# Where the Gram matrices of a gated delta rule are made, and how the blocks of its triangular solve reach the chip's memory

## The chip, the core and the metric

The kernel runs on one core of a Trainium2 chip. The metric is the device time of one execution in microseconds (us), from the first to the last instruction of the core. The engines are named as in the profile: PE (matrix products; PEld loads its weights), DVE (vector), ACT (scalar functions), POOL (GpSimd) and SP, which here only issues DMAs; ACT and POOL issue some too. TensorE's granted clock has two levels, 1.2 and 2.4 GHz.

## What is computed

A decoder layer on 1024 tokens of width 2048, all float32. After an RMS norm one projection feeds two groups of heads: a gated delta rule (8 heads of 128) and a sparse attention (8 query heads, 2 key/value heads) that keeps 256 keys per query by the scores of an indexer. Their gated outputs go through one output projection; the input is added, and a last RMS norm ends it. The change is in the delta rule, which works by blocks:

```
q = l2_normalize(q) * dk**-0.5 ;  k = l2_normalize(k)
gc    = cumsum(g)                                   # log decay inside a block
decay = where(incl, exp(gc_i - gc_j), 0)
lmat  = where(strict, (k * beta) @ k.T * decay, 0)  # "Gram", strictly lower
tmat  = inverse(lmat + eye)                         # the solve
w, u  = tmat @ (k * beta * exp(gc)), tmat @ (v * beta)
# then block after block: v_new, o and the state
```

Blocks here have 128 tokens. Each block's inverse is put together from two 64 x 64 diagonal blocks, which are solved directly, and the block below the diagonal.

## The kernel before

The activations h^T stay on chip, split into two exact parts (`hT`), and every projection is a slab of 256 columns (`slab_cm`, product at L286). A slab has 8 pieces of weights; a piece is loaded by SP (`wraw`, L200, three buffers), split by ACT (`whi`, L191) and POOL (`wlo`, L192, two buffers each) and gives 24 matmuls of 512 columns into four PSUM banks. There are 5664 such matmuls in all, in this order: small columns, four slabs of the indexer, five of the attention's queries and keys (`proj_qk`), four of the delta rule's keys ("k"), four of its queries ("q"), four of its values ("v"), four gate slabs of the attention and four of the delta rule. The output projection follows (L1276 to L1303).

A scheduler orders each engine's instructions when the program is built, by priorities: weights first, then the emptying of banks, then side work, then projection matmuls. Side work therefore stands between projection matmuls wherever the scheduler expects its inputs. On the chip each engine takes its instructions strictly in the order so made.

Side work, in its order: the indexer's scores; the choice of the 256 keys (`tally`, tiles `tj`, `cand`, `hit`, `key`; L652 to L681), a long chain on DVE during the last query slabs and the first two key slabs; attention (`attend`: logits `lgp`, then `pT`, `po`), which needs that choice and lies in the key, query and first value slabs; then the delta rule's part that needs no values; last the recurrence over the eight blocks (`delta_rule`).

A key, query or value slab (`proj_conv`) empties each of its banks with ACT into a stage tile `xr` (four buffers). ACT, DVE and POOL make the causal convolution and SiLU in place (`cy`, L700 to L705). In the next slab `tokens` transposes the result on PE (`ctok`, L711, in the trace under the helper L150) into the one PSUM bank with the tag "ev"; ACT reads it, for keys four times with a running sum of squares (`ssk`) and four times into the tile that goes to DRAM. The channels-first tile also goes to DRAM (`cT`).

The part that needs no values comes after attention, in tiles of memory that attention gave back. `pipelined` goes over 16 units of a block of 128 tokens and four heads. `gram_load` has SP load the keys (`kT`, L910) and the rows of gc, repeated on every partition (`gcb`, L905). `gram_unit` makes four products on PE (L916), four Relu and one Exp on ACT (L918, L919), a triangular select on POOL (L920), and four DVE operations (L922) that scale the product by `cn` = -beta rk^2 and by the decay; SP stores the result (`Ms`, L924). After both units of a block `block_load` (L932) has SP read the two diagonal 64 x 64 blocks of all eight heads back, one block per partition, in rows of 256 bytes. `solve` inverts all 128 blocks at once on DVE in 62 steps of two operations (`ut`, `mb`; L941, L943). `combine` makes the block below the diagonal, for which SP reads `L2bd` from `Ms` (L965).

A gate slab (`proj_gate`) empties a bank in two steps: ACT writes a tanh to a stage tile (`sz`, L1114), then DVE reads that tile and the bank (L1115).

## Time and profile before

| | us |
|---|---|
| median of 3 runs | 2167.59 |
| lowest and highest run | 2165.65, 2169.2 |
| span of the profiled execution | 2165.4 |

The page gives no other time of the profiled execution than its span. Busy shares of that span: PE 96%, PEld 81%, DVE 60%, ACT 40%, POOL 29%. The page cuts the span in 40 slices of 54.1 us and gives a digit for each, in tenths. A matmul's busy time has its pipeline in it, so that two that follow each other overlap in the records. "x <- y" after an idle time says what ended it.

### The profile page before, as it was taken

To read this page: it belongs to the slowest core of one execution; us is meant where nothing else is said; L and a number is where in the kernel's file an instruction comes from. 1 tells how busy PE (TensorE), PEld (TensorE's weight loads), DVE (VectorE), ACT (ScalarE), POOL (GpSimd) and SP (SyncE) were. 2 spreads that over 40 slices of the span, in tenths; PEclk is the share of its full clock that TensorE was granted. 3 is DMA by queue.
4 is the path that set the end of the run, shared out by engine and by line. 5 is a ranking of instruction groups with operands and counts; after the bars stand their busy time and mean duration, and the time that the engine had idled before them with its cause. 6 is when DMAs were issued, how large, how long until landed. Compare 5 with 4: busy or idle time off the path is not lost.

```text
span 2165.4 us, 30374 instructions
## 1 busy us (share of the span) xinstructions
PE 2084.5 (96%) x10529; PEld 1754.1 (81%) x10529; DVE 1293.9 (60%) x2751; ACT 872.3 (40%) x2054; POOL 637.9 (29%) x696
## 2 busy tenths in 40 slices
PE   7999999999999999999999978899999999999998
PEld 6888887877887888888888866778889877777887
DVE  8626766899999656545555426992154454445335
ACT  7425544211133655545545543112355433334223
POOL 6443334555532211112112222222233221111211
PEclk9999999999999999999999999999999999999999
DMA  6222232222223332222222395126565474556434
GB/s 191 72 71 78 71 81 78 65 77 68 70 80 112 111 88 87 73 78 81 67 72 74 108 199 106 61 80 169 167 195 182 136 252 136 160 160 223 140 121 157
DMA packets 258699, 248.93 MB, mean 115 GB/s; under 512 B 61888, under 2 KB 208752, under 8 KB 258096
## 3 DMA queue, kind: packets, MB, share of 16 engines
q1 hardware_dynamic: 205296, 187.19, 30.5%
q0 software_dynamic: 10240, 33.56, 5.1%
q10 hardware_dynamic: 43008, 26.22, 4.0%
q8 instruction: 83, 1.36, 0.3%
q14 instruction: 72, 0.59, 0.1%
HBM read 185.66 MB, written 61.24 MB: 114 GB/s over the span
## 4 chain that ended last, share of the span: by engine, by line
PE 53%; DVE 21%; DMA 5%; issue 2%; ACT 2%; SPq 1%; POOL 0%; DVEq 0%; ACTq 0%; POOLq 0%
PE cm L286 26%; PE to L1276 13%; DVE tj L652 8%; DVE mb L943 3%; DVE ut L941 3%; PE lgp L147 2%; PE po L147 2%; PE pT L150 1%; PE tl L1303 1%; DVE cy L702 1%; PE tm L238 1%; DMA Ms<-M 1%; DMA kT<-cTk 1%; PE ctok L150 1%; DVE sw L456 1%
## 5 line engine op out<-in xcount | busy, mean ns | idle before, releaser
L286 PE MATMUL cm<-hT,whi 128*128 128x512 f32 (+1 forms) x3776 | 1212.1, 396 | 16.4 <-DVE sz L1115 11.5
L286 PEld LDWEIGHTS cm<-hT,whi 128*128 128x128 f32 (+1 forms) x3776 | 709.1, 189 | 162.1 <-DVE sz L1115 13.7
L286 PE MATMUL cm<-hT,wlo 128*128 128x512 f32 (+1 forms) x1888 | 748.7, 397 | 5.3 <-POOL wlo L192 5.2
L192 POOL TENSOR_TENSOR wlo<-wraw,whi 128x512 fp32r<-128x512 f32 (+1 forms) x248 | 336.6, 1358 | 887.4 <-ACT whi L191 869.0
L286 PEld LDWEIGHTS cm<-hT,wlo 128*128 128x128 f32 (+1 forms) x1888 | 357.5, 189 | 80.2 <-POOL wlo L192 9.1
L191 ACT ACTIVATE whi<-wraw 128x512 fp32r<-128x512 f32 (+1 forms) x256 | 159.0, 621 | 456.8 <-PE cm L286 329.5
L1276 PE MATMUL to<-whi,mx 128*128 128x512 f32 x896 | 281.2, 395 | 5.2 <-DVE sz L1115 2.6
L1276 PEld LDWEIGHTS to<-whi,mx 128*128 128x128 f32 x896 | 169.2, 189 | 46.1 <-ACT whi L225 3.2
L652 DVE TENSOR_SCALAR_CACHE_REDUCE tj<-score,cand 128x384 bf16<-128x384 f32 (+2 forms) x198 | 187.1, 945 | 6.6
L1276 PE MATMUL to<-wlo,mx 128*128 128x512 f32 x448 | 176.1, 395 | 4.0 <-DVE wlo L226 4.0
L226 DVE TENSOR_TENSOR wlo<-wraw,whi 128x512 fp32r<-128x512 f32 x112 | 77.0, 690 | 145.3 <-ACT whi L225 145.1
L509 DVE SCALAR_TENSOR_TENSOR score<-rl,wi,score 128x512 f32<-128x512 f32 (+3 forms) x150 | 127.5, 859 | 30.1 <-ACT rl L501 23.5
L221 POOL DMA_DIRECT2D wraw<-in_w_out_dram x112 | 60.4, 539 | 255.3 <-DVE wlo L226 229.5
L225 ACT ACTIVATE whi<-wraw 128x512 fp32r<-128x512 f32 x112 | 70.1, 629 | 156.5 <-PE to L1276 132.2
L702 DVE SCALAR_TENSOR_TENSOR cy<-xr,convw,cy 128x512 f32<-128x512 f32 x144 | 119.9, 833 | 21.6 <-ACT cy L700 20.0
L794 DVE CUSTOM_DVE_ANT_0 lg<-lgp,mk 128x512 f32<-128x512 f32 (+3 forms) x96 | 53.2, 555 | 88.5 <-PE lgp L147 87.5
L1276 PEld LDWEIGHTS to<-wlo,mx 128*128 128x128 f32 x448 | 85.0, 190 | 23.7 <-DVE wlo L226 4.8
L813 DVE TENSOR_TENSOR pT<-pT 128x512 fp32r<-128x512 f32 (+1 forms) x80 | 49.7, 634 | 68.8 <-ACT pT L812 68.7
L501 ACT ACTIVATE rl<-isc 128x512 f32<-128x512 f32 (+1 forms) x105 | 58.9, 572 | 55.3 <-PE isc L147 30.9
L147 PE MATMUL po<-pT,vv 128*128 128x256 f32 x432 | 72.2, 285 | 0.0
L941 DVE TENSOR_TENSOR ut<-mb 128x62 f32<-128x62 f32 (+30 forms) x62 | 62.9, 1015 | 13.6 <-DMA mb<-Ms 11.8
L147 PEld LDWEIGHTS po<-pT,vv 128*128 128x128 f32 x432 | 65.2, 189 | 6.8
(280 smaller groups left out, 2614.4 us busy)
## 6 DMA issues: line engine op xcount, KB each, us to landing
wraw<-in_w_in_dram SPq DMA_DIRECT2D x232, 256.0 KB, 2.9
wraw<-in_w_out_dram POOLq DMA_DIRECT2D x128, 256.0 KB, 3.2
xt<-in_x_dram SPq DMA_DIRECT2D x32, 256.0 KB, 4.8
kT<-cTk SPq DMA_DIRECT2D x32, 256.0 KB, 3.1
szT<-sz SPq DMA_DIRECT2D x32, 256.0 KB, 2.1
mx<-oT SPq DMA_DIRECT2D x32, 256.0 KB, 4.1
mx<-szT SPq DMA_DIRECT2D x32, 256.0 KB, 6.3
ox<-in_x_dram SPq DMA_DIRECT2D x30, 256.0 KB, 3.2
```

The source lines that it names most:

```text
L147: return anchored(PE.matmul(*a, **k))
L191: S.activation(whi[:, :, :ncol], raw[:, :, :ncol], AF.Copy)
L192: eng.tensor_tensor(wlo[:, :, :ncol], raw[:, :, :ncol], whi[:, :, :ncol].bitcast(F32), op=ALU.subtract)
L225: last_w[:] = [S.activation(whi, raw, AF.Copy), V.tensor_tensor(wlo, raw, whi.bitcast(F32), op=ALU.subtract)]
L226: V.tensor_tensor(wlo, raw, whi.bitcast(F32), op=ALU.subtract)]
L286: mms.append(PE.matmul(bank[:n, :], w[:, k, g * P:g * P + n], h_ap(kt, a, slice(h * HT, h * HT + HT)), start=(p == 0 and k == 0 and i == 0 ...
L509: V.scalar_tensor_tensor(dst, r, w1, dst, op0=ALU.mult, op1=ALU.add)
L652: V.tensor_scalar(junk[:, :(b + 1) * P], score[b], cand[:, i:i + 1], 0.0, op0=op, op1=ALU.add, accum_out=cnt[:, i:i + 1])
L702: V.scalar_tensor_tensor(y, xr[:, j:j + HT], convw[:, j, ch:ch + 1], y, op0=ALU.mult, op1=ALU.add)
L941: V.tensor_tensor(tv, u[:, j + 1:, j:j + 1].to_broadcast([P, n, j]), u[:, j:j + 1, :j].to_broadcast([P, n, j]), op=ALU.mult)
L943: V.tensor_tensor(u[:, j + 1:, :j], u[:, j + 1:, :j], tv, op=ALU.add)
L1276: PE.matmul(banks[j], m_ap(KTS[m], a, slice((4 * hf + j) * P, (4 * hf + j + 1) * P)), ws[m][w], start=(m == 0 and i == 0), stop=(m == D // ...
```

## The change

- `decay_units` makes exp(gc_i - gc_j), strictly lower, for the 16 units, and keeps it in DRAM (`dec`). Its instructions are issued by `w_piece`: with each of the pieces 1 to 5 of a slab, from the first query slab of the attention on, one slot is taken from the list `per_piece`; a slot loads one unit's rows of gc and makes the decay of the unit before. The first Relu of a unit stands behind that piece's weight split on ACT. The tile `gce` has two buffers.
- `tokens` of a key slab loads the decay of its head and four blocks on SP (`decay_load`), and after the transposes `gram` makes the four products from the channels-first tile that is still on chip, into the bank with the tag "ev". It works `cn` out from the sums of squares at hand (three small DVE operations), scales with four DVE operations in place, and SP stores the two diagonal blocks to `Md`, in the order in which the solve takes them, and the block below the diagonal to `L2s`.
- `block_load` is four loads of 32 partitions by 16 KB, issued on ACT's queue; `combine` reads `L2s`.
- The loop over the units, `gram_load`, `gram_unit`, `pipelined` and `Ms` are gone; `cn` is no longer made after the key slabs; the two scratch tiles of `rsqrt` in the pool `gp` have one buffer instead of two.

```diff
+    per_piece = []
@@ w_piece
-            w_split(whi, wlo, raw, ncol, V if w2d is w_out else G)
+            ins = w_split(whi, wlo, raw, ncol, V if w2d is w_out else G)
+            if per_piece and 1 <= p <= 5:
+                per_piece.pop(0)(ins)
@@ proj_conv
+        def decay_load(f, h):
+            E = gcp[0].tile([P, NCH, P], F32, tag="gce", name="gce", bufs=2)
+            SP.dma_start(E, dec[:, f * NCH:(f + 1) * NCH, h, :])
+            return E
+
+        def gram(f, h, o, E):
+            cs = slice(f * NCH, (f + 1) * NCH)
+            pg = sd.tile([P, 512], F32, tag="ev", name="gram", bufs=1)
+            for c in range(NCH):
+                PE.matmul(pg[:, c * P:(c + 1) * P], o[:, c * P:(c + 1) * P], o[:, c * P:(c + 1) * P], start=True, stop=True)
+            r2 = gcp[0].tile([P, NCH, 1], F32, tag="gr2", name="gr2", bufs=2)
+            V.tensor_scalar(r2, ssk[:, cs, h:h + 1], 4 * EPS, None, op0=ALU.add)
+            V.reciprocal(r2, r2)
+            V.scalar_tensor_tensor(cn[:, cs, h:h + 1], r2, -1.0, beta[:, cs, h:h + 1], op0=ALU.mult, op1=ALU.mult)
+            for c in range(NCH):
+                V.scalar_tensor_tensor(E[:, c, :], pg[:, c * P:(c + 1) * P], cn[:, f * NCH + c, h:h + 1], E[:, c, :],
+                                       op0=ALU.mult, op1=ALU.mult)
+            for q in range(2):
+                sl = slice(64 * q, 64 * q + 64)
+                SP.dma_start(Md.rearrange("(q c h) r j -> q h r c j", q=2, h=HEADS)[q, h, :, cs, :], E[sl, :, sl])
+            SP.dma_start(L2s[:, cs, h, :], E[64:128, :, 0:64])
@@ block_load
-    def block_load(mb, c):
-        for q in range(2):
-            sl = slice(64 * q, 64 * q + 64)
-            SP.dma_start(mb[part(c, q):part(c, q) + HEADS], Ms[c][sl, :, sl].rearrange("r h j -> h r j"))
+    def block_load(mb):
+        for i in range(4):
+            sl = slice(32 * i, 32 * i + 32)
+            S.dma_start(mb[sl], Md[sl])
@@ order of the work
+    def decay_units():
...
+        def load(c, g):
+            def fn(ins):
+                E[c, g] = gcp[0].tile([P, 4, P], F32, tag="gce", name="gce", bufs=2)
+                SP.dma_start(E[c, g], gcrow[c * HEADS + 4 * g:c * HEADS + 4 * g + 4, :][None, :, :].to_broadcast([P, 4, P]))
+            return fn
+
+        def make(c, g):
+            def fn(ins):
+                t = E[c, g]
+                for h in range(4):
+                    r = S.activation(t[:, h, :], t[:, h, :], AF.Relu, bias=ngc[:, c, 4 * g + h:4 * g + h + 1])
+                    if h == 0:
+                        after(r, ins)
+                S.activation(t, t, AF.Exp, scale=-1.0)
+                G.affine_select(t, t, [[0, 4], [-1, P]], ALU.is_gt, 0.0, base=0, channel_multiplier=1)
+                SP.dma_start(dec[:, c, 4 * g:4 * g + 4, :], t)
+            return fn
...
+        per_piece.extend(slot(n) for n in range(len(units) + 1))
...
-        with tc.tile_pool(name="g1a", bufs=1, reuse_waits="tile") as g1a:
-            def unit(c, g, *a):
-                gram_unit(g1a, c, g, *a)
-                if g == 1:
-                    block_load(mb, c)
-            pipelined(UNITS, lambda c, g: gram_load(g1a, c, g), unit, 2)
+        block_load(mb)
```

How the engines' orders change, at three places. A row is one instruction, or several alike that follow each other: the line, the operation, out<-in, the output's shape. Line numbers of the changed kernel are its own.

DVE at the end of the choice of keys: `mk` of 384 columns is the last mask, `kT` and `qaT` are the keys and queries that attention's first logits take; before:

```order
L680 SCALAR_TENSOR_TENSOR mk<-eq,mk 128x384
L702 SCALAR_TENSOR_TENSOR cy<-xr,convw,cy 128x512 x3
L705 SCALAR_TENSOR_TENSOR xr<-xr,cy 128x512
L745 TENSOR_TENSOR kT<-kT 128x512 x2
L777 TENSOR_TENSOR qaT<-qaT 128x256 x2
```

and with the change:

```order
L736 SCALAR_TENSOR_TENSOR gce<-gram,cn,gce 128x128 x4
L692 SCALAR_TENSOR_TENSOR mk<-eq,mk 128x384
L714 SCALAR_TENSOR_TENSOR cy<-xr,convw,cy 128x512
L717 SCALAR_TENSOR_TENSOR xr<-xr,cy 128x512
L732 TENSOR_SCALAR gr_7437<-ssk 128x4
L733 RECIPROCAL gr_7437<-gr_7437 128x4
L734 SCALAR_TENSOR_TENSOR cn<-gr_7437,beta 128x4
L783 TENSOR_TENSOR kT<-kT 128x512 x2
L815 TENSOR_TENSOR qaT<-qaT 128x256 x2
```

Ahead of the split of keys and queries there are now, counted over the whole order, six sets of the three small operations and five sets of four that scale a Gram product. On PE the first logits stand behind 2373 projection matmuls (2363 before) and attention's last product behind 3963 (3990).

ACT in the query slabs of the attention (`gce` is the decay's tile, first with Relu, then with Exp), with the change:

```order
L194 ACTIVATE whi<-wraw 128x512
L1139 ACTIVATE gce<-gce,ngc 128x128
L1142 ACTIVATE gce<-gce 128x512
L1139 ACTIVATE gce<-gce,ngc 128x128 x3
L194 ACTIVATE whi<-wraw 128x512
```

and SP at the same place:

```order
L1144 DMA dec<-gce 128x512
L480 DMA qkT<-qk 32x512
L1132 DMA gce<-gcrow 128x512
L204 DMA wraw<-in_w_in_dram 128x2x256
L1144 DMA dec<-gce 128x512
```

Before, the weight splits follow each other there, with the emptying of a slab's banks between. Three Relu of a unit now stand ahead of a weight split, the fourth and the Exp behind it; on SP a load of gc's rows into a buffer stands behind the store that empties one.

DVE at the solve (`ut` and `mb` are its two operations of a step); before, at steps 17 and 18 with the first gate slab:

```order
L941 TENSOR_TENSOR ut<-mb 128x782
L1115 SCALAR_TENSOR_TENSOR sz<-sz,cm_12727 128x512
L943 TENSOR_TENSOR mb<-mb,ut 128x46x17
L1115 SCALAR_TENSOR_TENSOR sz<-sz,cm_12728 128x512
L941 TENSOR_TENSOR ut<-mb 128x810
L1115 SCALAR_TENSOR_TENSOR sz<-sz,cm_12729 128x512
```

and with the change at the same steps:

```order
L947 TENSOR_TENSOR ut<-mb 128x782
L949 TENSOR_TENSOR mb<-mb,ut 128x46x17
L947 TENSOR_TENSOR ut<-mb 128x810
L714 SCALAR_TENSOR_TENSOR cy<-xr,convw,cy 128x512
L949 TENSOR_TENSOR mb<-mb,ut 128x45x18
L714 SCALAR_TENSOR_TENSOR cy<-xr,convw,cy 128x512
```

Steps 18 to 27 now hold the convolution of the last value slab, and the first two gate slabs come at steps 32 and 49; before, three gate slabs came at steps 17, 33 and 51, and the last value slab's convolution ended at step 3. On PE the recurrence begins behind 4855 projection matmuls (5028 before) and ends behind 5331 (5511).

## Rows read from the trace of the kernel before

**Rows 1.** The page: busy us (share of the span) xinstructions, and the slices of DMA.

```profile
PE 2084.5 (96%) x10529; PEld 1754.1 (81%) x10529; DVE 1293.9 (60%) x2751; ACT 872.3 (40%) x2054; POOL 637.9 (29%) x696
...
DMA  6222232222223332222222395126565474556434
```

**Rows 2.** Windows: length, busy us (instructions) of each engine, PE clock, DMA share, GB/s.

```profile
650.00:700.00 50.00, 46.91 (x206) 38.13 (x204) 48.90 (x65) 18.26 (x55) 11.84 (x13) 0.97 0.32 98
...
800.00:850.00 50.00, 50.00 (x268) 42.63 (x267) 29.02 (x82) 26.63 (x75) 8.87 (x13) 1.00 0.27 78
...
1250.00:1300.00 50.00, 38.00 (x182) 30.88 (x180) 14.59 (x45) 23.51 (x62) 11.81 (x18) 0.90 0.99 187
1300.00:1350.00 50.00, 41.48 (x177) 33.88 (x178) 29.26 (x49) 15.91 (x40) 11.44 (x10) 0.93 0.57 108
```

**Rows 3.** Groups of PE's matmuls, 1230 to 1340 us: busy, mean ns, idle before.

```profile
L286 PE MATMUL cm<-hT,whi 128*128 128x512 f32 x180 | 60.5, 412 | 4.1 <-ACT whi L191 4.1
L286 PE MATMUL cm<-hT,wlo 128*128 128x512 f32 x90 | 37.5, 416 | 0.4 <-POOL wlo L192 0.4
L887 PE MATMUL gram<-kT 128*128 128x128 f32 x128 | 20.5, 316 | 16.7 <-DMA kT<-cTk 16.7
L150 PE MATMUL ctok<-ident,xr 128*128 128x128 f32 x24 | 4.1, 299 | 0.6 <-DVE xr L705 0.6
```

**Rows 4.** The chain in order of time: start us, us, what.

```profile
1252.59 9.10 DMA Ms<-M
...
1546.02 1.78 PE pa L887 x16
...
1736.11 10.04 PE cm L286 x44
```

**Rows 5.** Groups of PE's matmuls, 1340 to 1460 us, beside the solve.

```profile
L286 PE MATMUL cm<-hT,whi 128*128 128x512 f32 x301 | 98.1, 405 | 11.6 <-DVE sz L1115 11.5
L286 PE MATMUL cm<-hT,wlo 128*128 128x512 f32 x150 | 60.4, 402 | 0.0
```

**Rows 6.** Timeline, PE at the first gate slab beside the solve: start, us, idle before.

```profile
1359.23 0.79 PE L286 MATMUL cm<-hT,whi 128*128 128x512 f32 x1 [6.77 <-DVE sz L1115]
```

**Rows 7.** Timeline, DVE and then PE at attention's first logits.

```profile
704.30 0.96 DVE L777 TENSOR_TENSOR qaT<-qaT 128x256 fp32r<-128x256 f32 x2 [0.16 <-ACT qaT L776]
...
704.32 1.89 PE L147 MATMUL lgp<-kT,qaT 128*128 128x512 f32 x7
```

**Rows 8.** The Gram stage's operations by line: ns min/median/max, first and last start.

```profile
L918 ACT ACTIVATE M<-gcb,ngc x64: 385/388/411, 1234.2 to 1310.0; 128x128 f32<-128x128 f32 x64
...
L919 ACT ACTIVATE M<-M x16: 612/630/635, 1235.5 to 1310.4; 128x512 f32<-128x512 f32 x16
...
L920 POOL TENSOR_SCALAR_AFFINE_SELECT M<-M x16: 636/637/693, 1236.2 to 1311.1; 128x512 f32<-128x512 f32 x16
...
L922 DVE SCALAR_TENSOR_TENSOR M<-gram,cn,M x64: 334/341/351, 1237.4 to 1313.1; 128x128 f32<-128x128 f32 x64
```

**Rows 9.** DMA issues: queue, count, KB each, median us from issue to landing.

```profile
szT<-sz SPq DMA_DIRECT2D x32, 256.0 KB, 2.1
...
gcb<-gcrow SPq DMA_DIRECT2D x16, 256.0 KB, 7.8
Ms<-M SPq DMA_DIRECT2D x16, 256.0 KB, 6.5
...
gcd<-gcrow SPq DMA_DIRECT2D x16, 256.0 KB, 3.7
```

**Rows 10.** 400 to 600 us: all engines; DVE's small operations, 395 to 600; one undisturbed.

```profile
400.00:600.00 200.00, 195.48 (x844) 160.08 (x843) 191.34 (x415) 31.29 (x51) 107.15 (x90) 0.98 0.25 69
...
L661 DVE SCALAR_TENSOR_TENSOR cand<-key,flip 128x6 int32<-128x6 int32 x25 | 14.9, 594 | 0.9
...
L663 DVE TENSOR_SCALAR hit<-cnt 128x6 int32<-128x6 f32 x24 | 10.3, 430 | 0.8
...
609.37 0.17 DVE L663 TENSOR_SCALAR hit<-cnt 128x6 int32<-128x6 f32 x1
```

More of the change, by code (lines that the diff above doesn't have):

```diff
@@ L112, in rsqrt @@
     def rsqrt(pool, y, v, n):
-        t1 = pool.tile([P, n], F32, tag=f"rs1_{n}", name="rs1", bufs=2)
-        t2 = pool.tile([P, n], F32, tag=f"rs2_{n}", name="rs2", bufs=2)
+        bufs = 1 if pool is gp else 2
+        t1 = pool.tile([P, n], F32, tag=f"rs1_{n}", name="rs1", bufs=bufs)
+        t2 = pool.tile([P, n], F32, tag=f"rs2_{n}", name="rs2", bufs=bufs)
         V.tensor_single_scalar(t1.bitcast(I32), v.bitcast(I32), 1, op=ALU.logical_shift_right)
@@ L408, in hybrid_layer @@
     tok = {nm: dr.tile([T, HEADS * P], F32, name="tok" + nm) for nm in "kv"}
+    Md = dr.tile([P, 64, 64], F32, name="Md")
+    L2s = dr.tile([64, NB, HEADS, 64], F32, name="L2s")
+    dec = dr.tile([P, NB, HEADS, P], F32, name="dec")
+    gcp = []
     oT = dr.tile([P, 16, T], F32, name="oT")
@@ L628, in hybrid_layer @@
         cyp = cyp_cm.__enter__()
+        gcp_cm = tc.tile_pool(name="gcp", bufs=1, side="right", reuse_waits="tile")
+        gcp.append(gcp_cm.__enter__())
         with tc.tile_pool(name="tkp", bufs=1, reuse_waits="tile") as tkp, pri(P_SIDE):
@@ L706, in ev @@
             late.append(lambda: tokens(f, h, o))
+        def decay_load(f, h):
[18 more added lines that the diff above has]
+            SP.dma_start(L2s[:, cs, h, :], E[64:128, :, 0:64])
         def tokens(f, h, o):
+            E = decay_load(f, h) if nm == "k" else None
             pt = sd.tile([P, 512], F32, tag="ev", name="ctok", bufs=1)
@@ L716, in tokens @@
                     S.activation(sqj, pt[:, c * P:(c + 1) * P], AF.Square, accum_out=ss[:, f * NCH + c, h:h + 1])
+            if nm == "k":
+                gram(f, h, o, E)
             if nm != "q":
@@ L875, in attention @@
             todo.append(e)
-    Ms = [dr.tile([P, HEADS, P], F32, name=f"Ms{c}") for c in range(NB)]
     TTs = [dr.tile([64, HEADS, 64], F32, name=f"TTs{c}") for c in range(NB)]
@@ L888, in mm4 @@
         return ps.rearrange("p (h j) -> p h j", h=4)
-    def pipelined(units, load, work, ahead):
-        got = {}
-        for n, u in enumerate(units):
-            for m in range(n, min(n + ahead + 1, len(units))):
-                if m not in got:
-                    got[m] = load(*units[m])
-            work(*u, *got.pop(n))
-            got[n] = None
-    UNITS = [(c, g) for c in range(NB) for g in range(2)]
     def gc_rows(pool, tag, c, g, bufs):
@@ L906, in gc_rows @@
         return E
-    def gram_load(g1, c, g):
-        kT = g1.tile([P, 4, P], F32, tag="kT1", name="kT1", bufs=3)
-        SP.dma_start(kT, cT["k"][:, 4 * g:4 * g + 4, c * P:(c + 1) * P])
-        return kT, gc_rows(g1, "gcb", c, g, 3)
-    def gram_unit(g1, c, g, kT, E):
-        M = g1.tile([P, 4, P], F32, tag="M1", name="M1", bufs=3)
-        pg = mm4("gram", kT, kT)
-        for h in range(4):
-            S.activation(M[:, h, :], E[:, h, :], AF.Relu, bias=ngc[:, c, 4 * g + h:4 * g + h + 1])
-        S.activation(M, M, AF.Exp, scale=-1.0)
-        G.affine_select(M, M, [[0, 4], [-1, P]], ALU.is_gt, 0.0, base=0, channel_multiplier=1)
-        for h in range(4):
-            V.scalar_tensor_tensor(M[:, h, :], pg[:, h, :], cn[:, c, 4 * g + h:4 * g + h + 1], M[:, h, :],
-                                   op0=ALU.mult, op1=ALU.mult)
-        SP.dma_start(Ms[c][:, 4 * g:4 * g + 4, :], M)
     def part(c, q):
         return (q * NB + c) * HEADS
-    def block_load(mb, c):
-        for q in range(2):
-            sl = slice(64 * q, 64 * q + 64)
-            SP.dma_start(mb[part(c, q):part(c, q) + HEADS], Ms[c][sl, :, sl].rearrange("r h j -> h r j"))
+    def block_load(mb):
+        for i in range(4):
+            sl = slice(32 * i, 32 * i + 32)
+            S.dma_start(mb[sl], Md[sl])
     def solve(g1, mb):
@@ L1117, in proj_gate, with slot, fn @@
         slab_cm([(c0, CG)], CG, ev, budget=budget)
+    def decay_units():
+        E = {}
+        def load(c, g):
[14 more added lines that the diff above has]
+            return fn
+        units = [(c, g) for c in range(NB) for g in range(2)]
+        def slot(n):
+            def fn(ins):
+                if n < len(units):
+                    load(*units[n])(ins)
+                if n > 0:
+                    make(*units[n - 1])(ins)
+            return fn
+        per_piece.extend(slot(n) for n in range(len(units) + 1))
     kvp_cm = tc.tile_pool(name="kvp", bufs=1, side="right", reuse_waits="tile")
     kvp = kvp_cm.__enter__()
+    decay_units()
     for c in range(4):
@@ L1140, in hybrid_layer @@
     kvp_cm.__exit__(None, None, None)
+    gcp_cm.__exit__(None, None, None)
     proj_conv("v", C_GV, 0)
```

6 lines of the change are left out of this document (3 added, 3 removed).

## The prediction

> **What bounds the kernel now.** I read the page's busy shares and slices first [rows 1]: PE is busy 96% of the span, and the slices of DMA show a 9 and a 5 in places 24 and 25, 1245 to 1353 us, where it is else at 2 to 6. The busy time of a matmul contains its pipeline, so I price PE by spacing instead: 44 projection matmuls with 512 columns take 10.04 us in the chain of waits, 0.228 us each, and 16 of the 128-column fp32 ones 1.78 us, 0.111 us each [rows 4]. By that price a stretch such as 800 to 850 us is full: PE stands at 50.00 of 50, DVE at 29, ACT at 27, POOL at 9 [rows 2]. So almost everywhere the kernel is bound by PE, and a change saves time only where PE has holes.
>
> The largest hole is the Gram stage. Between 1230 and 1340 us PE issued 270 projection matmuls, 128 Gram and 24 transposing ones [rows 3]: 270 x 0.228 = 61.6 and 152 x 0.111 = 16.9, together 78.5 us of work in 110. **31.5 us are lost.** The rows name the wait: 16.7 us before gram for DMA kT<-cTk [rows 3]; the chain has a 9.10 us store Ms<-M [rows 4]; DMA stands at 0.99 and the granted clock at 0.90 in that window [rows 2], so part of the loss is PE running at the lower of its two levels (1.2 instead of 2.4 GHz) after it had idled.
>
> The second hole is beside the solve. Between 1340 and 1460 us PE issued 451 projection matmuls [rows 5], 102.8 us of work in 120: 17.2 us lost. Its waits are for DVE's sz, which reads a gate slab's bank and stands in DVE's order between steps of the solve; the first of them is 6.77 us [rows 6].
>
> **The change part by part.**
>
> *The Gram stage goes.* Its 64 Gram products (128 matmuls in the trace) cost PE the same 0.111 us elsewhere, so only the 31.5 us of waiting go: **-31.5**. With it go 64 loads and stores of 128 to 256 KB at the place where DMA is full. What is late next is the solve's block load: 2 MB in four issues on ACT's queue. At the lowest rate of 1300 to 1350 us, 108 GB/s [rows 2], it takes some 19 us, at the rate of 1250 to 1300, 187 GB/s, 11. That is off PE's path: PE has a whole value slab to do first. ACT's four issues are covered by the lead of one piece that the split weights have (24 x 0.228 = 5.5 us); if that cover went, they would cost about as long as a landing of 2.1 us [rows 9].
>
> *The Gram moves into the key slabs.* Attention's first logits wait for DVE, which is full up to there: 650 to 700 us shows 48.90 of 50 [rows 2]. DVE ended the split query at 705.26 and PE began logits at 704.32 on the first part [rows 7], so today the two meet. The order puts six sets of three small operations and five of four Gram products ahead of the split keys, with as many other operations as before: 18 x 0.2 (a 6-column operation takes 0.17 us [rows 10], with its gap 0.2) + 20 x 0.341 [rows 8] = 10.4 us. PE gets, ahead of the same logits, ten more projection matmuls (2373 instead of 2363) and six sets of four Gram products: 10 x 0.228 + 48 x 0.111 = 7.6 us. The other ten tiles of the Gram come after that, where DVE stands near 29 of 50: nothing, while DVE has that slack; without it each is 4 x 0.341 + 0.6 = 2.0 us, 20 in all.
>
> *The decay moves under the query projections.* Its 16 selects of 0.637 us on POOL [rows 8] add 10.2 us to POOL, which is busy 107 of 200 us there, beside a DVE at 191 [rows 10]. The row on DVE's small operations shows what POOL costs DVE: cand takes 594 ns in the mean and hit 430, where one undisturbed takes 170; 25 x 0.42 + 24 x 0.26 = 16.8 us for 107 us of POOL [rows 10], 0.157 us per us. For 10.2 us more that is 1.6 us. If every select held one DVE operation up for its whole length, it would be 16 x 0.637 = 10.2 us [rows 8]. I take 1.6, because the rows are of this very stretch, and keep 10.2 as a rival. A rule speaks against the change here: the Trainium skill (SBUF — State Buffer, section "Terms") says that DVE and GpSimd arbitrate for a shared port pair, that it is held for the whole instruction and that the loser fully blocks. By that rule the term would be the 10.2; the trace agrees that DVE's small operations wait beside POOL (594 for 170 ns), not that each POOL instruction meets one. Logits then come 10.4 + 1.6 - 7.6 = **+4.4** us of PE's time later.
>
> ACT's part of a decay, 4 x 0.388 + 0.630 = 2.18 us [rows 8], stands between two weight splits, with loads and stores ahead of it on SP, and it has two buffers. A store (2.1, as szT), a load (3.7, as gcd), ACT 2.18 and POOL 0.64 [rows 8, 9] make a loop of 8.6 us for every second decay; PE gives it two pieces, 2 x 5.47 = 10.9 us. So I take 0. With the landings of the crowded Gram stage, 6.5 and 7.8 [rows 9], the loop is 17.1 us; that end is the rival on the slower side. DMA stands at 0.25 here [rows 10], which is near the lower end. SP's waits for a store's landing hold the weight loads behind them, which run three buffers ahead.
>
> *Bank hand-over.* Of the third and fourth key slabs the last bank now comes right behind a Gram product, whose tile must be given back before ACT (0.6 us) can empty the bank. One of these lies ahead of the logits and is inside the 4.4; the other I put at **+1** (0 to 3).
>
> *The solve.* It starts about a value slab earlier. DVE now has the last value slab at its steps 18 to 27 and two gate slabs at 32 and 49, where before three gate slabs stood at 17, 33 and 51. A value slab's bank is emptied by ACT alone, so one of three waits goes: 17.2 / 3 = 5.7, taken as **-5**. Bounds: all 17.2 gone, or, if the solve starts late against the order, a further wait like the 6.77 us one [rows 6].
>
> The delta rule's first product then comes at projection matmul 4855 instead of 5028, and its last transposes leave 333 instead of 153. It stays covered, and PE's work behind it is the same.
>
> Sum: -31.5 + 4.4 + 1 - 5 = -31.1 us on the span of 2165.4, 2134.3. The span lies 2.2 us under the median of the runs, 2167.59; with that, **2136.5 us**.
>
> **The rivals.**
> 1. *Key tiles in a chain.* The transposes and the Gram share one bank: transposes, eight ACT reads, Gram, seven DVE operations between the tallies, next transposes. The order leaves about 57 projection matmuls (13 us) between two tiles. If the chain takes 2 us more than that for each of the eight tiles beside the top-k, PE loses 16 us, in which the 4.4 are contained: 2148. For it: transposes already waited for DVE's xr there. Against: DVE is never idle long there, so its order holds. 0.13.
> 2. *Every select blocks DVE.* 10.2 instead of 1.6: +8.6, 2145. For it: hit and cand do take several times their own length beside POOL [rows 10]. Against: the mean over the stretch. 0.07. It is the rule of the Trainium skill's page SBUF — State Buffer, named above, taken to the letter.
> 3. *The solve starts late.* The block load takes its 19 us, the last value slab's convolution stands 18 steps behind it on DVE, the transposes of its tokens wait on PE with the gate slab's matmuls queued behind, and none of the old waits goes: +6.8 instead of -5, 2148. For it: the old waits are just this. 0.09.
> 4. *Slower: the decay loop stalls the weights.* If the loop takes 17.1 us instead of 10.9, ACT waits in front of a weight split, PE behind it, and each of eight loops costs 6.2 us: 49.6, thus 2186. It decides from a loop of 14.8 us on (31.1 / 8 = 3.9 over 10.9). Against: DMA at 0.25, and three pieces in eight carry no decay, in which the loop catches up. 0.07.
> 5. *No gain.* The solve starts no sooner, or PE's hole at the end of attention only changes its owner: about 2166. Against: the blocks are in DRAM hundreds of us earlier, and in the order the solve starts at attention's end. 0.04.
>
> **How the numbers follow.** The forecast has 0.60. Its low end is all 17.2 us of the second hole gone and no loss in the key slabs: 2136.5 - 12.2 - 5.4 = 2119. The upper end takes rivals 1 and 3 added, 2136.5 + 11.6 + 11.8 = 2160. The range is 2119 to 2160; outside remain rivals 4 and 5 and small tails, under 0.2. A measurement tells about 0.2%, 4.3 us, from no change. Forecast and rivals 1 to 3 hold 0.89, of which 0.03 for several at once that eat most of the gain: faster 0.86, same 0.05, slower 0.09.
>
> **What would show it.** Right: no wait of PE for a Gram load, and between the end of attention and the solve PE issues near 44 projection matmuls in 10 us at a granted clock of 1.00; logits begin 10 to 14 us after 704; the first solve step comes 10 to 20 us behind attention's last product; sz waits on PE under 12 us; DVE's small operations in the choice of keys barely longer. Wrong: PE waiting for whi while ACT waits for gce between 400 and 580 us (rival 4), PE waiting for ctok or gram in the key slabs over 10 us (rival 1), or for xr or sz during the solve as long as now (rival 3).

## The result, and the profile after

The changed kernel takes 2148.99 us (median of 4 runs, 2148.49 to 2149.51) against 2167.14 for the kernel before; the ratio is 0.9916, 95% interval 0.9902 to 0.993. It is faster, by 18 us; 31 were forecast, and 2149 lies inside the range. The profiled execution has a span of 2147.7 us and a time of 2149.51.

The page of the kernel after, PE's line and the slices of DMA, answering to [rows 1]:

```profile
PE 2079.6 (97%) x10529; PEld 1749.6 (81%) x10529; DVE 1298.4 (60%) x2798; ACT 872.0 (41%) x2054; POOL 642.2 (30%) x696
...
DMA  6222223343224444222222242255665364556434
```

The 9 and the 5 in places 24 and 25 are now 4 and 2. The windows of [rows 2], after (length, busy us and instructions of PE, PEld, DVE, ACT, POOL, granted PE clock, DMA share, GB/s):

```profile
650.00:700.00 50.00, 45.78 (x212) 37.18 (x211) 49.65 (x90) 17.77 (x53) 13.04 (x12) 0.97 0.41 118
800.00:850.00 50.00, 50.00 (x289) 43.46 (x288) 31.40 (x85) 25.50 (x75) 8.20 (x8) 1.00 0.46 124
1250.00:1300.00 50.00, 47.96 (x218) 39.40 (x217) 40.58 (x51) 15.50 (x34) 13.39 (x13) 0.99 0.41 103
1300.00:1350.00 50.00, 43.26 (x183) 34.51 (x182) 49.48 (x45) 12.69 (x28) 13.53 (x8) 0.94 0.28 84
```

PE stands at 47.96 where it stood at 38.00. The groups of PE's matmuls from attention's end on, 1250 to 1360 us (busy, mean ns, idle before), answering to [rows 3]: no matmul waits for a load any more.

```profile
L292 PE MATMUL cm<-hT,whi 128*128 128x512 f32 x276 | 88.4, 401 | 4.8 <-DVE sz L1121 4.8
L292 PE MATMUL cm<-hT,wlo 128*128 128x512 f32 x138 | 55.3, 401 | 0.0
L151 PE MATMUL ctok<-ident,xr 128*128 128x128 f32 x28 | 4.4, 280 | 4.0 <-DVE xr L717 4.0
```

To compare kernels whose stages lie at other times, I count where PE stands in its order by the projection matmuls it has issued (5664 in all), and sum what PE loses in each stretch: from the start of each matmul to the start of the next, less the usual spacing of its kind in the traces (0.227 us for 512 columns, 0.111 for 128). Idle time and matmuls at the lower clock are both in it. Each kernel's profiled execution, us lost:

| kernel | start to 2016 | top-k's end, to 2400 | attention, to 3900 | Gram stage's place, to 4300 | beside the solve, to 4896 | beside the recurrence, to 5664 | output |
|---|---|---|---|---|---|---|---|
| before | 29.5 | 5.9 | 4.8 | 32.6 | 18.3 | 5.6 | 19.5 |
| **after** | 30.0 | 15.4 | 5.7 | 6.8 | 12.1 | 15.1 | 13.4 |
| e1 second gcd buffer | 30.7 | 12.2 | 6.4 | 7.1 | 12.7 | 2.3 | 16.2 |
| e2 two query slabs first | 29.1 | 9.0 | 5.5 | 6.7 | 14.8 | 8.3 | 18.2 |
| e3 solve's loads on SP | 33.0 | 14.6 | 5.8 | 6.1 | 13.4 | 14.5 | 19.2 |
| e4 before, new storage and loads | 29.0 | 6.0 | 4.8 | 12.0 | 14.8 | 9.2 | 15.7 |
| e5 before, loads' queue alone | 30.3 | 6.6 | 4.8 | 31.7 | 19.3 | 6.4 | 18.8 |
| e6 before, storage alone | 30.6 | 5.8 | 4.8 | 21.4 | 19.4 | 6.3 | 14.5 |
| e7 = e4 + second gcd buffer | 30.8 | 6.5 | 4.8 | 10.5 | 16.7 | 4.1 | 14.4 |
| e8 = e1 + e2 | 30.6 | 8.0 | 5.5 | 7.3 | 14.9 | 2.6 | 17.6 |
| e9 = e5, loads behind the last unit | 30.3 | 6.0 | 4.8 | 35.6 | 14.3 | 4.3 | 18.5 |
| e10 no products | 31.1 | 15.9 | 6.0 | 7.6 | 12.8 | 9.1 | 14.7 |
| e11 Gram moved, old storage | 32.0 | 14.2 | 5.7 | 24.4 | 12.5 | 7.1 | 15.2 |
| e12 first keys on ACT's queue | 30.2 | 14.5 | 6.7 | 7.4 | 12.4 | 3.2 | 16.8 |

So the change gave 25.8 us at the Gram stage's place and 6.2 beside the solve, and took back 9.5 at the end of the top-k search and 9.5 beside the recurrence. The output's 13.4 against 19.5 I do not count: over these fourteen profiles it goes from 13.4 to 19.5, and it is 13.4 and 19.2 in the kernel after and in e3, whose matmuls there stand in the same order. Whether any of it belongs to the change is open. A profile is one execution: e3's lies 5.9 us above the median of its runs and e8's 4.6 above, e7's 7.3, e11's 4.4 and e6's 4.1 below.

**The end of the search.** The rows of the kernel after, in time: DVE's last mask, SP's issues, PE's first logits.

```profile
706.96 0.55 DVE L692 SCALAR_TENSOR_TENSOR mk<-eq,mk 128x384 bf16<-128x384 bf16 x1
```
```profile
707.07 1.24 SPq L740 DMA_DIRECT2D Md<-gce  x2
708.36 1.00 SPq L741 DMA_DIRECT2D L2s<-gce  x1
709.47 0.54 SPq L693 DMA_DIRECT2D mask<-mk  x1
711.03 0.38 SPq L722 DMA_DIRECT2D gce<-dec  x1
712.73 0.32 SPq L781 DMA_DIRECT2D kT<-qkT  x1
```
```profile
720.27 0.79 PE L148 MATMUL lgp<-kT,qaT 128*128 128x512 f32 x1 [3.93 <-ACT qaT L814]
```

In the trace of before the last mask and SP's loads of the keys stood here:

```profile
696.41 0.54 DVE L680 SCALAR_TENSOR_TENSOR mk<-eq,mk 128x384 bf16<-128x384 bf16 x1
```
```profile
693.54 3.76 SPq L681 DMA_DIRECT2D mask<-mk  x2
697.39 0.41 SPq L200 DMA_DIRECT2D wraw<-in_w_in_dram  x1
697.89 0.93 SPq L743 DMA_DIRECT2D kT<-qkT  x2
```

DVE's last mask comes 10.55 us later, the keys' loads 14.8, the first logits 16 [rows 7]. With the change SP waited 1.2 us with the first of the keys' loads until the store of that mask had landed; before, it had no such wait.

**Beside the recurrence.** ScalarE's longest waits for the decay rows gcd, and what SP did meanwhile, after:

```profile
1605.86 1.28 ACT L1041 ACTIVATE A<-gcd,gc 128x128 f32<-128x128 f32 x4 [8.72 <-DMA gcd<-gcrow]
...
1622.39 1.28 ACT L1041 ACTIVATE A<-gcd,gc 128x128 f32<-128x128 f32 x4 [6.54 <-DMA gcd<-gcrow]
```
```profile
1609.53 0.37 SPq L1022 DMA_DIRECT2D qg<-cTq  x1
1614.93 0.38 SPq L204 DMA_DIRECT2D wraw<-in_w_in_dram  x1
1615.41 0.42 SPq L1020 DMA_DIRECT2D kT<-cTk  x1
1615.92 0.45 SPq L1030 DMA_DIRECT2D vb<-tokv  x1
1616.47 0.38 SPq L929 DMA_DIRECT2D gcd<-gcrow  x1
```

The sixth step of the recurrence takes 30.4 us from its first product to the next step's, where the third to fifth take 23.3 to 23.5 and the sixth took 24.9 before. The load of gcd stands on SP behind a weight piece that waits 5.0 us for its buffer, that is for POOL's split of an earlier piece.

### The profile page after: what moved, and what is told of

The parts are those of the page before. It is cut to its first block, busy times and chain, and to the rows that moved or that the text cites. A ratio compares the mean times of both kernels' runs of the same rounds, so it can differ in the third digit from the quotient of the medians.

```text
span 2147.7 us, 30435 instructions
## 1 busy us (share of the span) xinstructions
PE 2079.6 (97%) x10529; PEld 1749.6 (81%) x10529; DVE 1298.4 (60%) x2798; ACT 872.0 (41%) x2054; POOL 642.2 (30%) x696
## 4 chain that ended last, share of the span: by engine, by line
PE 51%; DVE 8%; DMA 5%; issue 2%; ACT 1%; SPq 1%; POOL 0%; DVEq 0%; ACTq 0%; POOLq 0%
PE cm L292 26%; PE to L1309 12%; PE lgp L148 3%; DVE ut L947 2%; PE po L148 2%; DVE mb L949 2%; PE pT L151 1%; DMA gcd<-gcrow 1%; DMA mx<-szT 1%; PE tl L1336 1%; PE tm L244 1%; PE ctok L151 1%; DVE cy L714 1%; DMA ox<-in_x_dram 1%; PE hh L923 0%
## 5 line engine op out<-in xcount | busy, mean ns | idle before, releaser
L292 PEld LDWEIGHTS cm<-hT,wlo 128*128 128x128 f32 (+1 forms) x1888 | 355.6, 188 | 85.0 <-POOL wlo L195 14.3
L519 DVE SCALAR_TENSOR_TENSOR score<-rl,wi,score 128x512 f32<-128x512 f32 (+3 forms) x150 | 127.9, 862 | 29.5 <-ACT rl L511 22.8
L714 DVE SCALAR_TENSOR_TENSOR cy<-xr,convw,cy 128x512 f32<-128x512 f32 x144 | 118.4, 822 | 22.5 <-ACT cy L712 20.1
L511 ACT ACTIVATE rl<-isc 128x512 f32<-128x512 f32 (+1 forms) x105 | 59.0, 571 | 55.7 <-PE isc L148 30.2
L1121 DVE SCALAR_TENSOR_TENSOR sz<-sz,cm 128x512 f32<-128x512 f32 x32 | 21.7, 682 | 90.8 <-ACT sz L1120 90.2
L148 PE MATMUL lgp<-kT,qaT 128*128 128x512 f32 (+3 forms) x288 | 70.4, 353 | 3.9 <-ACT qaT L814 3.9
```

Of the source, the lines that this page charges most:

```text
L148: return anchored(PE.matmul(*a, **k))
L292: mms.append(PE.matmul(bank[:n, :], w[:, k, g * P:g * P + n], h_ap(kt, a, slice(h * HT, h * HT + HT)), start=(p == 0 and k == 0 and i == 0 ...
L511: S.activation(rl[:, :w], ps2[:, :w], AF.Relu)
L519: V.scalar_tensor_tensor(dst, r, w1, dst, op0=ALU.mult, op1=ALU.add)
L714: V.scalar_tensor_tensor(y, xr[:, j:j + HT], convw[:, j, ch:ch + 1], y, op0=ALU.mult, op1=ALU.add)
```

## Experiments

Ratios are to the kernel before, run beside each, with the 95% interval.

**e1: a second buffer for the recurrence's decay rows.**

```diff
-                E = gc_rows(g2, "gcd", c, g, 1)
+                E = gc_rows(g2, "gcd", c, g, 2)
```


> The changed kernel with a second buffer for the decay rows of the recurrence (gcd), so that the next unit's load need not wait until the unit before has been multiplied. Theory (the recurrence now runs earlier, and the 9 us that TensorE loses beside the gate slabs are the wait for this load, which stands on SP behind a weight piece): ScalarE's wait for gcd falls from 65.7 us to under 25, the sixth step of the recurrence from 30.4 us to about 24, and the time from 2149 to 2140 to 2143. Rival (the stall is another link of the same ring, as the store of ot or the weight pieces, and only changes its name): 2147 to 2150 with TensorE's loss beside the gate slabs unchanged.

2137.8 us, 0.9868 (0.9856 to 0.9881), 11 us faster than the kernel after. What ScalarE and POOL waited for at this tile, in e1:

```profile
its engine sat idle before it (us, times) until:
  PE pog L1090: 31.8, 6
  PE hh L923: 24.0, 10
  ACT A L1041: 14.1, 3
  DMA gcd<-gcrow: 2.3, 1
```

In the kernel after the last of these rows was 65.7 us in 14 times. The sixth step takes 23.3 us, PE loses 2.3 us beside the recurrence instead of 15.1. The theory's signs came, and the time lies a little under its range. The edit also changed PE's order: it now has 50, 58, 51, 51, 54, 51 and 51 projection matmuls between the steps (e12 below has the counts of the other kernels). The buffer takes away ScalarE's wait for gcd, but how much of the 12.8 us it gives without the new order is not separated.

**e2: two query slabs ahead of the key slabs.**

```diff
-        slabs = [("k", i) for i in range(4)] + [("q", i) for i in range(4)]
+        slabs = [("q", 0), ("q", 1)] + [("k", i) for i in range(4)] + [("q", 2), ("q", 3)]
...
-            if n == 4:
+            if n == 6:
```


> The changed kernel with two query slabs of the delta rule ahead of its four key slabs, so that no Gram stands beside the end of the top-k search. Theory (the Gram's DVE work and its DMAs on SP push out the last masks and the loads of the first logits; 16 us lost there against 6.7 before): first logits about 10 us earlier against the matmuls ahead of them, the loss there 6 to 9 us, the time 2139 to 2143. Rival (the products cost the same wherever they stand, since DVE also sets the pace of the softmax beside attention): the loss appears in the 700 to 1000 us stretch instead, and the time is 2146 to 2152.

2142.65 us, 0.9893 (0.988 to 0.9906). First logits at 706.7 us instead of 720.3; PE loses 9.0 at the search's end instead of 15.4, and 5.5 in attention, where all the key slabs now are, against 4.8 in the kernel before, which makes no Gram there. So the Gram's work costs under 1 us beside attention and 6 us beside the search. Some of the gain is not this: the recurrence lost 8.3 instead of 15.1, and nothing in the edit touches it.

**e3: the solve's loads on SP.**

```diff
-            S.dma_start(mb[sl], Md[sl])
+            SP.dma_start(mb[sl], Md[sl])
```


> The changed kernel with the four loads of the solve's blocks on SP's queue instead of ACT's: one part of the change undone. Theory (at that place the blocks lie in DRAM for 380 us already and both queues only pass the loads on): 2147 to 2151, first solve step within 4 us of 1263. Rival (SP stands behind weight pieces that wait for buffers, so the loads leave 5 to 10 us later or hold the weights back): 2153 to 2158. It also serves to see whether the 30.4 us step of the recurrence comes again in another profile.

2151.02 us, 0.9929 (0.9914 to 0.9943); first solve step at 1263.8 instead of 1263.0. Where nothing else happens, the queue of these four loads is worth nothing. The sixth step of the recurrence took 30.1 us again: it belongs to this kernel's order and is no accident of one execution.

**e4: the kernel before with the storage and the loads of the change; the Gram stays a stage.**

```diff
-        SP.dma_start(Ms[c][:, 4 * g:4 * g + 4, :], M)
+        for q in range(2):
+            sl = slice(64 * q, 64 * q + 64)
+            SP.dma_start(Md[part(c, q) + 4 * g:part(c, q) + 4 * g + 4].rearrange("h r j -> r h j"), M[sl, :, sl])
+        SP.dma_start(L2s[:, c, 4 * g:4 * g + 4, :], M[64:128, :, 0:64])
...
             pipelined(UNITS, lambda c, g: gram_load(g1a, c, g), unit, 2)
+            block_load(mb)
```


> The kernel before with the storage alone: its own Gram stage stays where it was, but stores into the solve's order, and the blocks come in four loads on ACT's queue after the last unit. Theory (the gain is that the Gram's chain no longer stands on TensorE, the storage is worth next to nothing): 2162 to 2170. Rival (the 16 strided loads on SP, which held weights and Gram units back, were a good part of the loss of the stage): 2150 to 2160.

2142.1 us, 0.9891 (0.9875 to 0.9906). My theory is refuted, and the time lies below the rival's range too: **without moving the Gram at all, the storage and the four loads give as much as the whole change**, rather more, though the two intervals just overlap. The stage loses 12.0 us of PE instead of 32.6. Its windows in e4 (columns as above):

```profile
1250.00:1270.00 20.00, 18.44 (x101) 15.25 (x99) 5.97 (x22) 9.81 (x27) 5.66 (x7) 1.00 0.87 215
1270.00:1290.00 20.00, 15.34 (x88) 12.70 (x87) 9.08 (x21) 13.09 (x32) 6.44 (x11) 1.00 0.91 227
```

The DMA engines are still nearly full, but move 215 to 227 GB/s, where before it was 187 between 1250 and 1300 us [rows 2]; M's stores and the decay rows land sooner (Md 3.3 us and gcb 5.4 in the median, Ms 6.5 and gcb 7.8 before [rows 9]), so ScalarE no longer waits 23.6 us in five times for a free M, but 13.5 in four. In the trace of before, the units' waits and the full DMA stood in one stretch, and I had not taken them apart.

**e5 and e6: the two halves of that, alone.** e5 keeps the old storage and puts the 16 loads on ACT's queue, in the program after the units; e6 has the new storage and leaves 16 loads on SP, each pair behind its stores.

```diff
-            SP.dma_start(mb[part(c, q):part(c, q) + HEADS], Ms[c][sl, :, sl].rearrange("r h j -> h r j"))
+            S.dma_start(mb[part(c, q):part(c, q) + HEADS], Ms[c][sl, :, sl].rearrange("r h j -> h r j"))
...
-                if g == 1:
-                    block_load(mb, c)
             pipelined(UNITS, lambda c, g: gram_load(g1a, c, g), unit, 2)
+            for c in range(NB):
+                block_load(mb, c)
```


> The kernel before with the place of the loads alone: Ms stored as before, and the same 16 strided loads of the solve's blocks, but on ACT's queue after the last Gram unit. Theory W (the stage's loss came from SP, where a load that waits for its store holds the weight pieces and the next units' loads behind it): 2140 to 2148, TensorE's loss in the stretch of the Gram stage 10 to 15 us against 33 before. Theory D (the loss came from the strided form of the loads, which only the new storage removes): 2156 to 2167.

2167.28 us, 1.0 (0.9991 to 1.001): theory W is refuted; the queue alone is worth nothing. The loads went out between 1251.9 and 1327.8 us, beside the units as before, so this run does not show what a later place would give. e5's windows show full DMA engines that move little:

```profile
1250.00:1270.00 20.00, 13.67 (x70) 11.63 (x71) 3.40 (x13) 8.79 (x27) 3.74 (x5) 0.88 1.00 190
1270.00:1290.00 20.00, 12.44 (x49) 9.75 (x49) 3.27 (x12) 5.31 (x17) 2.51 (x3) 0.76 1.01 151
```

The stores of e6 are those of e4; its loads, against the kernel before:

```diff
     def block_load(mb, c):
         for q in range(2):
-            sl = slice(64 * q, 64 * q + 64)
-            SP.dma_start(mb[part(c, q):part(c, q) + HEADS], Ms[c][sl, :, sl].rearrange("r h j -> h r j"))
+            sl = slice(part(c, q), part(c, q) + HEADS)
+            SP.dma_start(mb[sl], Md[sl])
```


> The kernel before with the new storage alone: the units store in the solve's order, but each token block's two loads stay where they were, on SP behind their stores. Theory W: 2160 to 2172, loss of the stage 27 to 38 us, since three stores a unit stand on SP and the loads wait as before. Theory D: 2140 to 2150.

2157.4 us, 0.9952 (0.9939 to 0.9965), between the two expectations: the storage alone gives 9 us, and with four loads on ACT's queue in place of 16 on SP (e4) 25. Neither W nor D holds alone. Why the stage still loses 21.4 is not shown. Between 1250 and 1310 us the DMA engines are as full as before without any load in 256-byte rows (0.92 to 0.98, at 172 to 194 GB/s), and ScalarE waits 20.1 us for M's stores; e4 differs from e6 in the queue, the place and the number of the loads at once.

**e7 and e8: both repairs, and a better kernel.** e7 is e4 with e1's buffer, e8 is the changed kernel with the edits of e1 and e2.

> The kernel of the fourth run (before with storage and loads of the change, Gram where it was) with a second buffer for the recurrence's decay rows. If the recurrence's stall there (3.9 us as it starts and 3.1 us in its fourth and fifth steps) is the wait for these rows: 2134 to 2139. If it is not: 2140 to 2144.

2145.0 us (2137.68 to 2149.02), 0.9892 (0.9875 to 0.991): no gain over e4. Its profile shows 4.1 us lost beside the recurrence instead of 9.2, but the times do not, and they spread over 11 us; I leave it as undecided.

> The changed kernel with both repairs: two query slabs ahead of the key slabs, and the second buffer of decay rows. If the two losses are separate: 2130 to 2136. If the query slabs' gain was mostly the recurrence falling otherwise: 2136 to 2140. Against the seventh run it tells what moving the Gram is worth by itself once its costs are repaired: faster by 2 to 7 us if the Gram stage's remaining loss (12 us against 7) is what it saves, equal or slower if the key slabs give it back.

2134.37 us, **0.9847 (0.9832 to 0.9863)**: faster than both kernels, by 32 us than the one before. Against e4 and e7 (0.9891 and 0.9892), moving the Gram is worth some 10 us by the medians once its two costs are repaired, more than the 2 to 7 expected. The profiled executions of e7 and e8 do not show it (spans of 2136.0 and 2137.3 us), so where these 10 us come from is open.

**e9: e5 with the loads held behind the last unit.** The edit against the kernel before:

```diff
-        S.activation(M, M, AF.Exp, scale=-1.0)
+        last_e.append(S.activation(M, M, AF.Exp, scale=-1.0))
...
-            SP.dma_start(mb[part(c, q):part(c, q) + HEADS], Ms[c][sl, :, sl].rearrange("r h j -> h r j"))
+            after(S.dma_start(mb[part(c, q):part(c, q) + HEADS], Ms[c][sl, :, sl].rearrange("r h j -> h r j")), last_e[-1])
```


> The fifth run again, with its 16 strided loads (old storage, ACT's queue) held behind the exponentials of the last Gram unit; there they had still gone out one by one between the units, from 1252 to 1328 us. Theory P (what costs is a load's transfers beside the units' own: they keep the DMA engines full, so the units' stores land in 6 to 10 us and hold the three M buffers): without them among the units the stage loses 10 to 17 us of TensorE, the solve starts no later than in the fourth run by more than 12 us, and the time is 2142 to 2152. Theory S (what costs is the units' stores in the old form, whatever the loads do): 2160 to 2170, ScalarE's wait for M's stores still over 20 us.

2160.76 us, 0.9969 (0.9955 to 0.9983). The Gram units now run better (9.0 us lost between the 3900th and the 4128th projection matmul, 18.2 before), so half of theory P holds; but the loads then stand alone and cost the same again. The time lies in theory S's range, but S's sign did not come: ScalarE waits 15.2 us for M's stores, not over 20. Each holds ACT's queue 2.1 us in the median, 32.4 us in all, with the weight splits behind them. The windows in which they run:

```profile
1290.00:1310.00 20.00, 12.40 (x46) 9.37 (x44) 5.35 (x14) 3.14 (x5) 2.09 (x2) 0.83 0.76 94
1310.00:1330.00 20.00, 10.72 (x26) 7.86 (x27) 4.62 (x7) 4.88 (x12) 1.28 (x1) 0.59 0.74 83
```

**e10: no products in the key slabs.**

```diff
-            for c in range(NCH):
-                V.scalar_tensor_tensor(E[:, c, :], pg[:, c * P:(c + 1) * P], cn[:, f * NCH + c, h:h + 1], E[:, c, :],
-                                       op0=ALU.mult, op1=ALU.mult)
+            V.tensor_copy(E[:, 0, 0:1], pg[:, 0:1])
```


> The changed kernel without the four products a half slab that scale the Gram by the decay on DVE (a copy of one column of the Gram stands in their place, so the blocks hold the decay alone); decay loads, stores and the three small DVE operations stay. If DVE's products beside the top-k search are what pushes out the first logits: TensorE's loss between the 2208th and the 2400th projection product falls from 14.5 to 7 to 9 us, 2139 to 2145. If it is SP, whose stores of blocks and loads of decay stand ahead of the loads for the logits: the loss stays at 12 us or more, 2146 to 2150.

2147.94 us, 0.9914 (0.9902 to 0.9927). First logits come at 712.8, 7.5 us sooner (twenty products by 0.341 are 6.8 [rows 8]), yet PE loses as much, 15.9: the program's order moved the logits forward on PE by as much (2344 projection matmuls stand ahead of them instead of 2373, and 29 x 0.228 is 6.6 us). By the numbers this is the second expectation, SP; e12 shows that reading to be wrong too.

**e11: the Gram moved, with the old storage.**

```diff
-                SP.dma_start(Md.rearrange("(q c h) r j -> q h r c j", q=2, h=HEADS)[q, h, :, cs, :], E[sl, :, sl])
-            SP.dma_start(L2s[:, cs, h, :], E[64:128, :, 0:64])
+            SP.dma_start(Ms[:, cs, h, :], E)
...
+                SP.dma_start(mb[part(c, q):part(c, q) + HEADS], Ms[sl, c, :, sl].rearrange("r h j -> h r j"))
```


> The changed kernel with the old storage: the Gram is made in the key slabs, but its blocks are stored by token and head as before, and the solve reads them with 16 strided loads on SP. If moving the Gram and storing in the solve's order each remove the same loss, so that their gains overlap: 2147 to 2156, at most the loads' longer landing worse than the change (first solve step within 12 us of 1263). If the storage is needed also when the Gram is moved (the loads hold SP, and with it the weight pieces, as the solve starts): 2157 to 2166.

2165.87 us, 0.9997 (0.9988 to 1.0007). The counterpart of e4: **moving the Gram alone gives nothing**, as the second expectation has it. The first solve step comes at 1289.4 us, 26 later than in the change, and PE loses 24.4 us at the place where the stage was. That is 8.2 less than before, and the search's end takes 8.3 back (14.2 against 5.9). SP's issues in e11:

```profile
1247.94 0.37 SPq L204 DMA_DIRECT2D wraw<-in_w_in_dram  x1
1248.41 13.45 SPq L935 DMA_DIRECT2D mb<-Ms  x7
1261.96 2.37 SPq L204 DMA_DIRECT2D wraw<-in_w_in_dram  x1
1264.38 18.45 SPq L935 DMA_DIRECT2D mb<-Ms  x9
```

The same 2 MB leave ACT's queue in the kernel after as four issues in 1.59 us:

```profile
1250.78 1.28 ACTq L938 DMA_DIRECT2D mb<-Md  x3
...
1252.71 0.31 ACTq L938 DMA_DIRECT2D mb<-Md  x1
```

What DMA moved meanwhile, first in e11 (1247 to 1285 us), then after (1247 to 1265):

```profile
DMA packets 10503, 3.54 MB, mean 93 GB/s; under 512 B 8057, under 2 KB 10502, under 8 KB 10502
```
```profile
DMA packets 2333, 3.55 MB, mean 197 GB/s; under 512 B 159, under 2 KB 2204, under 8 KB 2204
```

As many bytes, those of other transfers among them, took 38 us in place of 18. The old loads fetch rows of 64 numbers, 256 bytes, 8192 in all. The Trainium skill (DMA: Bandwidth & Descriptors, section "Why small descriptors are slow (HBM only)") puts the overhead of a 256-byte descriptor at 27%. The trace agrees in the direction only: the rate falls to less than half, 93 of 197 GB/s. The packets of the loads show the same: in e11 the 8192 of 256 bytes took 42 ns each in the mean, 21.7 us of the time of all 16 DMA engines, and after the 128 of 16 KB that carry these bytes took 1215 ns each, 9.7 us. The two kernels differ in the queue and the number of the loads as well. For the queue e3 shows nothing; the number is not separated from the rows' length.

**e12: attention's first keys and queries on ACT's queue.**

```diff
-                SP.dma_start(lo.bitcast(F32), qkT[:, NHQ + g, sl])
+                (S if g == 0 else SP).dma_start(lo.bitcast(F32), qkT[:, NHQ + g, sl])
...
-            SP.dma_start(qT[:, 1].bitcast(F32), qkT[:, h0:h0 + 2, b * P:(b + 1) * P])
+            (SP if len(heads) > 1 else S).dma_start(qT[:, 1].bitcast(F32), qkT[:, h0:h0 + 2, b * P:(b + 1) * P])
+            heads.append(b)
```


> The changed kernel with the loads of the first key head and of the first two query tiles of attention on ACT's queue, so that they do not stand on SP behind the Gram's stores and decay loads. If SP's queue is what makes the first logits wait (ScalarE's split keys waited for these loads and TensorE 4.2 us for the split query): that wait goes, TensorE's loss between the 2208th and the 2400th projection product falls from 14.5 to 9 to 11 us, 2143 to 2146. If only the owner of the wait changes (DVE, whose last masks come 10 us later than before, or the mask's own load): loss 13 us or more, 2147 to 2151.

The loss stays, 14.5 us, and the first logits come at 721.9: not SP's queue, the wait changes its owner. ACT's rows in e12:

```profile
712.41 0.85 ACTq L781 DMA_DIRECT2D kT<-qkT  x2
713.31 0.28 ACT L752 ACTIVATE sqj<-ctok 128x128 bf16<-128x128 f32 x1 [4.29 <-DMA mask<-mk]
```

The loads leave at 712.4 from ACT's queue and left at 712.7 from SP, each time when the last mask, issued at 709.5, had landed: either queue stood for that store. So the chain here is DVE's last mask, its store behind the Gram's three, its landing, the keys. Yet the time is 2141.67 us, 0.9899 (0.9883 to 0.9914), outside both expectations. That is 7 us under the kernel after by the times, but some 4 by the ratios, whose intervals overlap: the kernel before took 2164.44 beside this run. By the profile the gain is the recurrence's: PE loses 3.2 us there instead of 15.1, though ScalarE still waits 41.2 us for gcd. PE has 51, 47, 51, 51, 54, 58 and 51 projection matmuls between its steps in e12, as in the kernel before, and 53, 48, 51, 51, 52, 51 and 54 in the kernel after and in e3. With one gcd buffer, some orders stall and some don't; with two (e1, e8) the stall was gone, in orders of their own.

## Why the prediction was right, and where not

- **"The Gram stage goes: -31.5."** Measured -25.8. The size was near, the reason was not. I read PE's waits for Gram loads, the 9.10 us store and a DMA share of 0.99 [rows 2 to 4] as the price of having the stage there, and booked all of it to the move. e11 and e4 show that the move with the old loads gives 0 and the storage with its four loads 25: a large part of that price was the solve's 16 loads in 256-byte rows. They were not all that filled the DMA engines: between 1245 and 1330 us before, the packets of these loads took 0.28 of the engines' time, all packets 0.92. The step that failed is "only the 31.5 us of waiting go". I priced the new load of 2 MB (11 to 19 us; it took 12, from 1250.8 to the first step at 1263.0) and never the old one, which stood in the same order. So it is in good part luck that 2149 lies inside the range, and near the 2148 of rivals 1 and 3: the same move with the old loads took 2165.87 us (e11), above the range.
- **What stayed at that place, 6.8 us.** 31.5 supposed none. Some 4.0 are waits for DVE, which now has the solve there (ctok for xr in the groups above), and 1.5 are matmuls at the lower clock right behind the first of these waits, 0.43 us apart instead of 0.227. The sz wait of 4.8 in the same groups comes behind the 4300th projection matmul and counts to the solve.
- **"Logits +4.4, bank +1."** Measured +9.5. The DVE part was right: 10.4 us of operations were listed, and the last mask comes 10.55 later. The 7.6 us of PE work were right too: its matmuls ahead of the logits are 7.2 us more. What failed is the silence on what follows the mask, which is the rest of the 16 us, some 5: three Gram stores ahead of the mask's store on SP, and keys that can be loaded only when the mask has landed (before, SP issued them 0.6 us behind the issue of the last mask). Logits came 16 us later, not 10 to 14. Rival 1 put the loss at 16 us; 9.5 lies between that and the 5.4 forecast, nearer to the forecast, and its sign, PE waiting over 10 us for ctok or gram, did not come: those waits are about 2 us.
- **"For 10.2 us more [of POOL] that is 1.6 us", rival 2.** Measured 0. POOL is busy 114.98 us between 400 and 600 instead of 107.15 [rows 10], and DVE's small operations cost what they did:

```profile
L673 DVE SCALAR_TENSOR_TENSOR cand<-key,flip 128x6 int32<-128x6 int32 x25 | 15.1, 602 | 0.9
...
L675 DVE TENSOR_SCALAR hit<-cnt 128x6 int32<-128x6 f32 x24 | 9.9, 411 | 0.8
```

- **"The decay loop: 0", rival 4.** Right. ScalarE waits for the decay's loads, but in time that it has: PE loses 30.0 us up to the 2016th projection matmul instead of 29.5. The ScalarE wait over 400 to 600 us, after:

```profile
ACT gce L1139 <- DMA gce<-gcrow: 59.1, 14, 6.5
```

- **"The solve, -5", rival 3.** Measured -6.2, and sz waits on PE 5.7 us in all instead of 11.5 [rows 5]. The first step comes 15 us behind attention's last product (1247.8 to 1263.0), inside the 10 to 20.
- **"The delta rule stays covered."** Measured +9.5, the largest error of any term. I counted projection matmuls behind the recurrence and did not ask whether its one-buffer loads still fit between its steps in the new order. [rows 9] has the row, gcd with 3.7 us from issue to landing, and I used it for the decay only.

In sum -31.1 was forecast for the span and -17.7 came. Of the 13.4 between, 5.7 are missing at the stage's place, 4.1 were lost at the logits and 9.5 beside the recurrence; some 6 came back in the output, which the profile of e3 does not show, and the rest are single us.

Open: which part of the Gram's work in the key slabs costs the 6 us that e2 takes back. The products make the logits 7.5 us later (e10), but an order laid out without them loses as much.

## What to carry to other kernels

When a stage stands still with the DMA engines full, price every transfer in it by bytes and by the length of its rows before booking the loss to the stage: rewriting a store so that the load behind it reads long rows, and issuing that load as four on another queue, gave here 25 us, where moving the work with the old loads gave nothing. A load in a one-buffer ring beside in-order queues is covered or bare depending on the order around it, so after any change that moves it, ask for its wait again; a second buffer can be worth trying: e1 gained 11 us with it, e7 nothing that the times show. Work put ahead of a stage's last store also delays whatever reuses that store's memory.

## What the runs showed of the hardware

- Of 16 loads issued one behind the other, each of 128 KB in 512 rows of 256 bytes, one held its queue 2.1 us in the median, on SP (e11) as on ACT (e9), and DMA was at a share of 0.74 to 0.81 with 83 to 125 GB/s. The first two in e11 held it only 0.39 and 0.60 us. Issued in pairs between other work the same loads held it 0.40 us (before) and 0.39 (e5); loads of as many bytes from whole blocks, in pairs too, 0.29 (e6).
- Stores in 256-byte pieces did not hurt in this way: e4 has more packets under 512 bytes in 1230 to 1330 us than the kernel before (13950 and 9324) and loses 20 us less. A 256-byte packet of the stores took 18 to 19 ns in the mean (e4, e6), one of the loads 42 to 46 (before, e5, e9, e11).
- 7.8 us more of POOL beside a full DVE did not lengthen DVE's small operations: 602 and 411 ns after, 594 and 430 before.
